# Entry of a hybrid mLSTM/attention kernel: latent norm factors first, dummy products moved, modulation columns amid a tile's products

## The chip, the cores and the metric

One NeuronCore of one Trainium2 chip runs the program. The metric is device time in microseconds of one execution; the median of three executions of the kernel before is 1206.87 us (1203.84 to 1209.22).

## What is computed

Two layers over 512 latent tokens and 256 context tokens with 1024 features: layer 0 is a bidirectional chunkwise mLSTM, layer 1 a banded windowed attention with sinks. Each layer first normalises and modulates its input, then projects it. For the entry of layer 0, which is all that the change touches, the reference is:

```python
mod_lat = jax.nn.silu(c) @ ada_w[layer] + ada_b[layer]
mod_ctx = jax.nn.silu(c_ctx) @ ada_w[layer] + ada_b[layer]
sh_l, sc_l, g_l = jnp.split(mod_lat[:, None, :], 3, axis=-1)
sh_c, sc_c, g_c = jnp.split(mod_ctx[None, None, :], 3, axis=-1)
h_lat = modulate(x, norm_g[layer], sh_l, sc_l)
h_ctx = modulate(ctx, norm_g[layer], sh_c, sc_c)
...
def rms_norm(a, g):
    af = af * lax.rsqrt(jnp.mean(af * af, axis=-1, keepdims=True) + EPS)
def modulate(a, g, shift, scale):
    return rms_norm(a, g) * (1 + scale) + shift
...
q, k, v, o, z, g = jnp.split(h @ w_in, ML_SPLITS, axis=-1)
```

## The kernel before

Features lie on the partitions and tokens on the free dimension. The input stands in eight feature tiles `x[j]` of 128 features by 768 tokens (`T`), of which 512 are latent (`TL`) and 256 context. Products are made in three passes of two-part numbers (`mm3`, line 188): high weight by high input, high by low, low by high. `HL` holds the modulated latent input in both parts, `HC` that of the context.

A scheduler sets the order of instructions on each engine from the order in the source and its own costs; `after(...)` (line 181) holds an instruction back until a named one has been issued. Each engine then works through its own list in that order, and SP issues the transfers.

The entry goes in these steps.

- **Dummies and sums of squares** (lines 246 to 265). `warm` runs products of zeros on TensorE, 36 of them into `pstat`. ScalarE squares the tiles, VectorE adds the squares in three groups of tiles, (0 to 3), (4, 5), (6, 7), and a product with `ones` sums each group over the partitions into `pstat`.
- **Norm factors** (`rs`, line 271, and `rsqrt`, line 194): one scale-and-add on VectorE, `Ln` and `Exp` on ScalarE, then three VectorE operations that refine the root. It is done for the 512 latent tokens (`rs(0, TL)`) and the 256 context tokens (`rs(TL, T)`), and gives `rstd`.
- **Modulation of layer 0** (`mod_quarter`, line 216). The vectors of two feature tiles (a quarter) come at once. Eight products with `ccol` make *rows* (line 221) from four 512 KB pieces of `ada0`, ScalarE copies the rows to `rt` (line 223), four products with `sel2` turn them into *columns* (line 225), and three small VectorE operations (lines 228 to 231) write shift and scale to `modc`. Quarter 0 is made before the first tile; quarter `c` is made ahead of tile `j = 1, 3, 5`, for the tiles after it.
- **Tiles** (line 307). For each `j`, VectorE multiplies `x[j]` by `rstd` (`xr`, line 314), ScalarE applies scale and shift (line 284) and casts to the high part (line 100), VectorE subtracts for the low part (line 106), and TensorE makes 12 latent products of 512 columns and 12 context products of 256 columns for the q and k weights of head 0 (lines 192 and 331), in three PSUM tiles `pqk`.
- **Gates** (lines 333 to 335): 48 products into `pgate`. VectorE's long gate chain (from line 362) starts with the last of them.

The weights come as `wraw` (SP), are cast to `whi` by ScalarE (line 100), and `wlo` is subtracted by VectorE (line 106), so ScalarE and VectorE do the weights' work in the same lists as the entry's own. `wraw` has two buffers: SP's third load of it waits until VectorE has made the first `wlo`.

A second lot of `warm`, 8 dummies into the first `pqk` (line 292), stands in TensorE's list between the sums of the first group and those of the second.

Of the kernel before, what the change touches and what calls it, by code (L numbers as in the profile page):

```python
# [8 lines left out]
F32 = mybir.dt.float32  # L9
# [7 lines left out]
P = 128  # L17
D = 1024
KT = D // P
TL = 512  # L20
TC = 256
T = TL + TC
# [4 lines left out]
NEG = -30000.0  # L27
BIG = -(2.0**100)

WARM, WARM2 = 36, 8  # L30


HEAD0 = "ooodommommommommodd"
# [31 lines left out]
def hybrid_kernel(ctx: ExitStack, tc: tile.TileContext, a: dict, out: bass.AP, dbg=None):  # L65
    nc = tc.nc
    ve, se, ge, te, sy = nc.vector, nc.scalar, nc.gpsimd, nc.tensor, nc.sync
# [8 lines left out]
    def mk(pool, shape, dt, tag, bufs=1, name=None):  # L76
        cnt[0] += 1
        return pool.tile(shape, dt, tag=tag, bufs=bufs, name=f"{name or tag}{cnt[0]}")
# [4 lines left out]
    def t0(shape, dt, tag, bufs=1):  # L83
        return mk(sb0, shape, dt, tag, bufs)

    def big(name):
        return mk(ps0, [P, 1024], F32, "big", 3, name)

    def ch(name):
        return mk(ps0, [P, 1024], F32, "ch", 1, name)  # L90

    def tmp(n=T, dt=F32):
        return t0([P, n], dt, "tmp", 5)

# [32 lines left out]
    def load_x(small=()):  # L127
        xs = [t_([P, 4, T], F32, n) for n in ("xa", "xb")]
        for j in range(KT):
            sy.dma_start(xs[j // 4][:, j % 4], a["xin"][:, j])  # L130
            for dst, src in small[j : j + 1]:
                sy.dma_start(dst, src)
        return xs, [xs[j // 4][:, j % 4] for j in range(KT)]

    _, x = load_x(small)
# [12 lines left out]
    st0 = [ada0(0)]  # L148
# [12 lines left out]
    sel2 = t0([P, 2], F32, "sel2")  # L161
# [19 lines left out]
    def after(*insts):  # L181

        st = ExitStack()
        for i in insts:
            st.enter_context(tc.issue_after(getattr(i, "ins", i)))
        return st

    def mm3(outs, w, ms, first, last):

        for i, (s, m) in enumerate(PASSES):  # L190
            for o, mv in zip(outs, ms):
                te.matmul(o, w[s], mv[m], start=first and i == 0, stop=last and i == 2)  # L192

    def rsqrt(dst, v, y, w, prev=None, tiny=0.0):

# [17 lines left out]
                out=junk, in0=src, in1=c2[:, v], scale=1.0, scalar=0.0,  # L213
                op0=ALU.mult, op1=ALU.add, accum_out=modc[:, layer, part, j, v : v + 1])

    def mod_quarter(R, srcs, c):


        for kk in range(2):
            for g in range(4):  # L220
                te.matmul(R[32 * g : 32 * g + 32], ccol[:, 4 * kk + g], srcs[4 * kk + g], start=kk == 0, stop=kk == 1)
        rt = tmp()[:, 0:TL]
        se.copy(rt, R)
        for q in range(4):
            te.matmul(R[:, 2 * q : 2 * q + 2], rt[:, q * P : (q + 1) * P], sel2, start=True, stop=True)
        js = slice(2 * c, 2 * c + 2)
        p4 = R[:, 0:8].rearrange("p (r j v) -> p r j v", r=2, v=2)
        ve.tensor_add(modc[:, 0, 0, js], p4[:, 0], adab[:, 0, 0, js, None].to_broadcast([P, 2, 2]))
        m = modc[:, 0, 1, js]
        ve.tensor_add(m, p4[:, 1], bp1[:, 0, js, None].to_broadcast([P, 2, 2]))  # L230
        ve.tensor_mul(m, m, ng[:, 0, js, None].to_broadcast([P, 2, 2]))

    HL = HC = None

# [11 lines left out]
    def warm(dst, n):  # L246
        for _ in range(n):
            te.matmul(dst[:, 0:TL], zeror, zeror[:, None, :].to_broadcast([P, 4, P]), start=True, stop=True)

    warm(pst, WARM)  # L250
    lastadd = []
    for js in ((0, 1, 2, 3), (4, 5), (6, 7)):
        for j in js:
            q = tmp()
            lastsq = se.activation(q, x[j], AF.Square)
            if j == 1:
                se.activation(csil, csil, AF.Silu)
                ve.tensor_copy(ccol[:, :, 0:2], csil.rearrange("p v k -> p k v"))
            if j == js[0]:
                ss = q  # L260
            else:
                with after(*lastadd):
                    lastadd = [ve.tensor_add(ss, ss, q)]
        for l, r in ((0, TL), (TL, T)):
            laststat = te.matmul(pst[:, l:r], ones, ss[:, l:r], start=(j == 3), stop=(j == 7))
    with after(*lastadd):
        ve.tensor_scalar(bp1, adab[:, :, 1], 1.0, None, op0=ALU.add)
    rstd = t0([P, T], F32, "bc0")
    v_, y_, w_ = tmp(), tmp(), tmp()

    def rs(l, r, prev=None):
        ve.tensor_scalar(v_[:, l:r], pst[:, l:r], 1.0 / D, EPS, op0=ALU.mult, op1=ALU.add)
        return rsqrt(rstd[:, l:r], v_[:, l:r], y_[:, l:r], w_[:, l:r], prev)

    rstd_exp, _ = rs(0, TL, lastsq)
    rs(TL, T)
    R = ch("R")
    mod_quarter(R[:, 0:TL], st0[0], 0)
    HL = t_([P, 2, KT, TL], F32R, "HL")
    HC = t_([P, 2, KT, TC], F32R, "HC")  # L280

    def enter(j, v, xr, hf):
        l, r = ((0, TL), (TL, T))[v]
        se.activation(hf[:, l:r], xr[:, l:r], AF.Identity,
                      scale=modc[:, 0, 1, j, v : v + 1], bias=modc[:, 0, 0, j, v : v + 1])
        dst = (HL, HC)[v]
        split(hf[:, l:r], dst[:, 0, j], dst[:, 1, j])

    wgt = t0([P, 3072], F32R, "s")
    acc = [big("pqk") for _ in range(3)]  # L290
    pbw = t0([P, 1024], F32R, "pb")
    warm(acc[0], WARM2)
    wq = [[load_w(a["w0"][0, u, 0]), None] for u in range(2)]
    st0.append(ada0(1))
    wq[0][1] = load_w(a["w0"][0, 0, 1])
# [10 lines left out]
    lastmm = None  # L306
    for j in range(KT):
        if j % 2 and j < KT - 1:

            c = j // 2 + 1  # L310
            with after(lastmm):
                mod_quarter(R[:, c % 2 * TL : c % 2 * TL + TL], st0[c], c)
        xr, hf = tmp(), tmp()
        ve.tensor_mul(xr, x[j], rstd)
        enter(j, 0, xr, hf)
        enter(j, 1, xr, hf)
        st, sp = j == 0, j == KT - 1
        hl, hc = hparts(j)
        wj = [[[wq[u][j // 4][m][:, j % 4, f * P : (f + 1) * P] for m in range(2)] for f in range(2)] for u in range(2)]
        for u in range(2):  # L320
            for f in range(2):
                mm3((acc[u][:, f * TL : (f + 1) * TL],), wj[u][f], [hl], st, sp)
        if j == 0:

            for u in range(2):
                te.matmul(acc[2][:, u * TL : (u + 1) * TL], zeror, zeror[:, None, :].to_broadcast([P, 4, P]),
                          start=True, stop=False)
        for u in (1, 0):
            for f in range(2):
                for i, (wi, m) in enumerate(PASSES):  # L330
                    lastmm = te.matmul(acc[2][:, u * TL + f * TC : u * TL + (f + 1) * TC], wj[u][f][wi], hc[m],
                                       start=False, stop=sp and f == 1 and i == 2)
# [361 lines left out]
    s = scores(qk)  # L694
# [39 lines left out]
    first = [gates.last, scores.last]  # L734
    for what in HEAD0:
# [25 lines left out]
    for h in range(1, NH0):  # L761
# [3 lines left out]
        s = scores(qk)  # L765
# [62 lines left out]
    for u in range(4):  # L828
        hi, lo = (w3a[:, 2 * u], w3a[:, 2 * u + 1]) if u < 3 else (w3b[:, 0], w3b[:, 1])
# [450 lines left out]
```

## Time and profile before

| what | value |
|---|---|
| median of 3 executions | 1206.87 us (1203.84 to 1209.22) |
| the profiled execution's own time | 1208.84 us |
| its span in the trace | 1207.0 us |
| mean granted TensorE clock | 0.983 |
| TensorE products, busy | 1151.3 us (95%) |
| VectorE, ScalarE, GpSimd, busy | 766.9, 541.1, 230.1 us |

The profiled execution lies 1.97 us above the median. The first 88 us, up to the last gate product, hold the steps above. Busy time of an engine is the time in which at least one of its instructions ran; the granted clock is 1.00 at 2.4 GHz and 0.50 at 1.2 GHz. In lists by time, a row gives the start, the duration, the engine and line, and in brackets the idle time of the engine before it with what ended that idle time; the durations of instructions that follow each other overlap a little.

### The profile page before, as it was taken

What the parts mean: (1) busy time and instruction counts of PE and PEld (TensorE: products, weight loads), DVE (VectorE), ACT (ScalarE), POOL (GpSimd) and SP (SyncE); (2) the same over time, 40 slices, a digit from 0 to 9 for tenths busy, and PEclk for the clock granted to TensorE, in tenths of its full rate; (3) what the DMA queues carried; (4) which work ended last, traced back from release to release, by engine and by line L of the source; (5) the groups of instructions that cost most, each with busy time, mean ns of one, the idle gap of its engine ahead of it and who ended that gap; (6) DMA issues with size and microseconds to landing.
All of it is one profiled execution on the core that took longest, in us unless ns stands there. A gap on an engine that the chain in (4) does not pass through costs nothing. (4 is left out here: it accounts for less than half of the span.)

```text
span 1207.0 us, 15997 instructions
## 1 busy us (share of the span) xinstructions
PE 1151.3 (95%) x6289; PEld 972.6 (81%) x6289; DVE 766.9 (64%) x1184; ACT 541.1 (45%) x901; POOL 230.1 (19%) x203
## 2 busy tenths in 40 slices
PE   7898899999999999999999999999999799998997
PEld 5677788888878888887888887888998587776776
DVE  4438878174845941582863367274777287979886
ACT  5443523343444232433423333443675277765663
POOL 0010520143201102211200330110233214123220
PEclk9998899999999999999999999999999899999999
DMA  8522522232215322221532112324108722225002
GB/s 311 196 70 70 199 77 74 79 102 81 81 53 182 111 70 71 71 66 47 201 122 70 60 55 70 122 70 123 53 21 170 189 84 65 70 71 140 18 18 70
DMA packets 38459, 116.90 MB, mean 97 GB/s; under 512 B 5088, under 2 KB 9328, under 8 KB 37360
## 3 DMA queue, kind: packets, MB, share of 16 engines
q1 hardware_dynamic: 35568, 108.55, 27.4%
q0 software_dynamic: 2816, 7.34, 3.4%
q8 instruction: 49, 0.80, 0.3%
q14 instruction: 26, 0.21, 0.1%
HBM read 107.60 MB, written 8.27 MB: 96 GB/s over the span
## 5 line engine op out<-in xcount | busy, mean ns | idle before, releaser
L100 ACT CAST whi<-wraw 128x1024 fp32r<-128x1024 f32 x102 | 107.0, 1052 | 202.6 <-PE pwo L192 51.4
L106 POOL TENSOR_TENSOR wlo<-wraw,whi 128x1024 fp32r<-128x1024 f32 x31 | 75.3, 2436 | 278.5 <-ACT whi L100 269.6
L106 DVE TENSOR_TENSOR wlo<-wraw,whi 128x1024 fp32r<-128x1024 f32 x71 | 87.5, 1234 | 54.0 <-ACT whi L100 54.0
L192 PE MATMUL po<-HL,whi 128*128 128x512 f32 x256 | 96.9, 402 | 0.0
L192 PE MATMUL pz<-HL,whi 128*128 128x512 f32 x256 | 96.3, 400 | 0.0
L192 PE MATMUL pqk<-HL,whi 128*128 128x512 f32 x240 | 90.3, 410 | 5.6 <-ACT HL L100 5.2
L192 PE MATMUL pv<-whi,HL 128*128 128x512 f32 x256 | 83.1, 391 | 0.0
L192 PE MATMUL po<-HC,whi 128*128 128x256 f32 x256 | 72.3, 282 | 0.0
L192 PE MATMUL pz<-HC,whi 128*128 128x256 f32 x256 | 71.9, 281 | 0.0
L192 PE MATMUL Lq<-HL,whi 128*128 128x512 f32 (+1 forms) x192 | 55.8, 370 | 6.2 <-DVE szt L1047 6.2
L1115 PE MATMUL Lpv<-PT,V 128*128 128x512 f32 x144 | 54.4, 430 | 7.2 <-DVE PT L106 6.0
L192 PEld LDWEIGHTS pqk<-HL,whi 128*128 128x128 f32 x240 | 46.1, 195 | 18.0 <-ACT HL L100 5.5
L192 PEld LDWEIGHTS po<-HL,whi 128*128 128x128 f32 x256 | 48.8, 190 | 12.6
L192 PEld LDWEIGHTS pz<-HL,whi 128*128 128x128 f32 x256 | 48.5, 190 | 12.4
L192 PEld LDWEIGHTS pv<-whi,HL 128*128 128x128 f32 x256 | 48.1, 188 | 11.3 <-DVE vgb L106 1.2
L614 POOL TENSOR_TENSOR tmp<-tmp,tmp 128x768 f32<-128x768 f32 x8 | 14.7, 1838 | 212.4 <-ACT tmp L613 212.4
L192 PE MATMUL pqk<-HC,whi 128*128 128x256 f32 x192 | 53.6, 279 | 0.0
L1080 DVE TENSOR_REDUCE negm<-Lsc 128x2 f32<-128x1024 f32 (+1 forms) x32 | 43.4, 1355 | 14.5 <-PE Lsc L1078 13.7
L212 DVE CUSTOM_DVE_ANT_0 junk<-qkp 128x1024 bf16<-128x1024 f32 x40 | 48.7, 1218 | 5.1 <-DMA qkp<-ada 4.6
L192 PE MATMUL po<-HL,wlo 128*128 128x512 f32 x128 | 51.8, 405 | 0.0
L192 PE MATMUL pz<-HL,wlo 128*128 128x512 f32 x128 | 51.6, 403 | 0.0
L106 DVE TENSOR_TENSOR PT<-LT,PT 128x512 fp32r<-128x512 f32 x72 | 48.9, 684 | 4.2 <-ACT PT L100 3.9
(388 smaller groups left out, 3247.3 us busy)
## 6 DMA issues: line engine op xcount, KB each, us to landing
wraw<-w SPq DMA_DIRECT2D x85, 512.0 KB, 3.6
qkp<-ada SPq DMA_DIRECT2D x30, 512.0 KB, 5.5
wraw<-wo SPq DMA_DIRECT2D x24, 512.0 KB, 3.5
vgb<-ada SPq DMA_DIRECT2D x9, 512.0 KB, 7.3
vga<-ada SPq DMA_DIRECT2D x8, 512.0 KB, 8.5
Q<-hl POOLq DMA_DIRECT2D x8, 512.0 KB, 5.5
xa<-xin SPq DMA_DIRECT2D x8, 384.0 KB, 4.2
xb<-xin SPq DMA_DIRECT2D x8, 384.0 KB, 6.3
```

Of the source, the lines that this page charges most:

```text
L100: se.copy(dst, src)
L106: return (le or ve).tensor_sub(lo, src, f32(hi))
L192: te.matmul(o, w[s], mv[m], start=first and i == 0, stop=last and i == 2)
L212: ve.tensor_tensor_reduce(out=junk, in0=src, in1=c2[:, v], scale=1.0, scalar=0.0, op0=ALU.mult, op1=ALU.add, accum_out=modc[:, layer, part ...
L614: (ge if e < 3 else ve).tensor_add(ss, ss, sq)
L1080: ve.tensor_reduce(nmx[:, 0, 2 * p2 : 2 * p2 + 2], both, axis=AX.X, op=ALU.max, negate=True)
L1115: te.matmul(po, V[:, kb, g], hl[:, m], start=(bi == 0 and m == 0), stop=(bi == len(blocks) - 1 and m == 1))
```

## The change

It does five things.

- `rs(0, TL)` stays where it is in the source, `rs(TL, T)` goes behind the first tile's latent input: the factors of the context are held back by `after(xr0, hi_0)`. The latent part of `xr` for tile 0 is a multiplication of its own (512 columns).
- The sums of squares go in two groups of four tiles, in place of three.
- `mod_quarter` is cut into `mod_rows` (rows and the copy) and `mod_cols` (columns and `modc`). Quarter 0 has a PSUM tile of its own, `R0`, of the kind that `pqk` uses.
- For `j = 1, 3, 5`, `mod_cols` is issued behind the first unit's (q) six latent products of that tile, in place of ahead of the tile.
- The second dummies are 16 in place of 8, and stand behind the columns of quarter 0.

```diff
-WARM, WARM2 = 36, 8
+WARM, WARM2 = 36, 16
...
-    def mod_quarter(R, srcs, c):
+    def mod_rows(R, srcs):
...
         rt = tmp()[:, 0:TL]
         se.copy(rt, R)
+        return rt
+
+    def mod_cols(R, rt, c):
+
         for q in range(4):
-            te.matmul(R[:, 2 * q : 2 * q + 2], rt[:, q * P : (q + 1) * P], sel2, start=True, stop=True)
+            mm = te.matmul(R[:, 2 * q : 2 * q + 2], rt[:, q * P : (q + 1) * P], sel2, start=True, stop=True)
...
+        return mm
...
-    for js in ((0, 1, 2, 3), (4, 5), (6, 7)):
+    for js in ((0, 1, 2, 3), (4, 5, 6, 7)):
...
+    R0 = big("R0")[:, 0:TL]
+    rt = mod_rows(R0, st0[0])
     rstd_exp, _ = rs(0, TL, lastsq)
-    rs(TL, T)
-    R = ch("R")
-    mod_quarter(R[:, 0:TL], st0[0], 0)
+    xr_0, hf_0 = tmp(), t0([P, T], F32, "rowt")
+    xr0 = ve.tensor_mul(xr_0[:, 0:TL], x[0][:, 0:TL], rstd[:, 0:TL])
+    cols0 = mod_cols(R0, rt, 0)
...
-        split(hf[:, l:r], dst[:, 0, j], dst[:, 1, j])
+        hi = se.copy(dst[:, 0, j], hf[:, l:r])
+        ve.tensor_sub(dst[:, 1, j], hf[:, l:r], f32(dst[:, 0, j]))
+        return hi
+
+    hi_0 = enter(0, 0, xr_0, hf_0)
+    with after(xr0, hi_0):
+        rs(TL, T)
+        ve.tensor_mul(xr_0[:, TL:T], x[0][:, TL:T], rstd[:, TL:T])
+        enter(0, 1, xr_0, hf_0)
...
-    warm(acc[0], WARM2)
+    with after(cols0):
+        warm(acc[0], WARM2)
+    R = ch("R")
+    R = [R[:, 0:TL], R[:, TL : 2 * TL]]
...
             with after(lastmm):
-                mod_quarter(R[:, c % 2 * TL : c % 2 * TL + TL], st0[c], c)
-        xr, hf = tmp(), tmp()
-        ve.tensor_mul(xr, x[j], rstd)
-        enter(j, 0, xr, hf)
-        enter(j, 1, xr, hf)
+                rt = mod_rows(R[c % 2], st0[c])
+        if j:
+            xr, hf = tmp(), tmp()
+            ve.tensor_mul(xr, x[j], rstd)
+            enter(j, 0, xr, hf)
+            enter(j, 1, xr, hf)
...
-                mm3((acc[u][:, f * TL : (f + 1) * TL],), wj[u][f], [hl], st, sp)
+                lastmm = mm3((acc[u][:, f * TL : (f + 1) * TL],), wj[u][f], [hl], st, sp)
+            if not u and j % 2 and j < KT - 1:
+                with after(lastmm):
+                    mod_cols(R[c % 2], rt, c)
```

From the last gate product on, the lists of all engines hold the same instructions in the same order as before, and SP's and GpSimd's lists are the same throughout. What moves stands at three places.

**Place 1, ScalarE's list from the load of its table to the first tile's latent input.** The table is that of `Ln` and `Exp`; `R_199` and `R_185` are the rows of quarter 0, `tmp_184` and `tmp_183` the root, `tmp_271` and `rowt_204` the modulated tile 0. Before:

```order
L199 ACT_TABLE_LOAD
L201 ACTIVATE tmp_184<-tmp_183 128x512
L203 ACTIVATE tmp_184<-tmp_183 128x256
L204 ACTIVATE tmp_184<-tmp_184 128x512
L204 ACTIVATE tmp_184<-tmp_184 128x256
L223 COPY tmp_208<-R_199 128x512
L100 CAST whi_234<-wraw_232 128x1024
L284 ACTIVATE tmp_271<-tmp_270,modc_113 128x512
L100 CAST whi_240<-wraw_238 128x1024
L100 CAST HL_217<-tmp_271 128x512
```

And now:

```order
L200 ACT_TABLE_LOAD
L224 COPY tmp_194<-R_185 128x512
L100 CAST whi_252<-wraw_250 128x1024
L202 ACTIVATE tmp_183<-tmp_182 128x512
L205 ACTIVATE tmp_183<-tmp_183 128x512
L100 CAST whi_258<-wraw_256 128x1024
L292 ACTIVATE rowt_204<-tmp_203,modc_113 128x512
L295 CAST HL_213<-rowt_204 128x512
L204 ACTIVATE tmp_183<-tmp_182 128x256
L205 ACTIVATE tmp_183<-tmp_183 128x256
```

`Ln` and `Exp` of the latent tokens (lines 202 and 205) now stand behind the copy of the rows and behind the first weight's cast; those of the context come behind the latent input.

VectorE's list at the same place, from the first scale-and-add of the factors. Before:

```order
L272 TENSOR_SCALAR tmp_183<-pstat_115 128x512
L272 TENSOR_SCALAR tmp_183<-pstat_115 128x256
L205 TENSOR_TENSOR tmp_185<-tmp_184 128x512
L205 TENSOR_TENSOR tmp_185<-tmp_184 128x256
L206 SCALAR_TENSOR_TENSOR tmp_185<-tmp_185,tmp_183 128x512
L206 SCALAR_TENSOR_TENSOR tmp_185<-tmp_185,tmp_183 128x256
L207 SCALAR_TENSOR_TENSOR bc_182<-tmp_185,tmp_184 128x512
L207 SCALAR_TENSOR_TENSOR bc_182<-tmp_185,tmp_184 128x256
L228 TENSOR_TENSOR modc_113<-R_199,adab_72 128x4
L230 TENSOR_TENSOR modc_113<-R_199,bp_114 128x4
L314 TENSOR_TENSOR tmp_270<-xa_76,bc_182 128x768
L231 TENSOR_TENSOR modc_113<-modc_113,ng_73 128x4
```

And now:

```order
L278 TENSOR_SCALAR tmp_182<-pstat_115 128x512
L233 TENSOR_TENSOR modc_113<-R_185,adab_72 128x4
L235 TENSOR_TENSOR modc_113<-R_185,bp_114 128x4
L236 TENSOR_TENSOR modc_113<-modc_113,ng_73 128x4
L106 TENSOR_TENSOR wlo_253<-wraw_250,whi_252 128x1024
L206 TENSOR_TENSOR tmp_184<-tmp_183 128x512
L207 SCALAR_TENSOR_TENSOR tmp_184<-tmp_184,tmp_182 128x512
L106 TENSOR_TENSOR wlo_259<-wraw_256,whi_258 128x1024
L208 SCALAR_TENSOR_TENSOR bc_181<-tmp_184,tmp_183 128x512
L285 TENSOR_TENSOR tmp_203<-xa_76,bc_181 128x512
L278 TENSOR_SCALAR tmp_182<-pstat_115 128x256
L296 TENSOR_TENSOR HL_213<-rowt_204,HL_213 128x512
```

`modc` and two low weight parts (`wlo`) now stand ahead of the end of the root (line 208) and of `xr` (line 285); before, both `wlo` came behind them.

**Place 2, TensorE's list between tile 0 and tile 1, and ScalarE's beside it.** `R_199` and `R_249` are the rows of quarter 1. TensorE before:

```order
L221 MATMUL R_199<-vgb_67,ccol_71 32x512 x4
L221 MATMUL R_199<-qkp_68,ccol_71 32x512 x4
L225 MATMUL R_199<-sel_109,tmp_313 128x2 x4
L192 MATMUL pqk_220<-HL_217,whi_234 128x512
L192 MATMUL pqk_221<-HL_217,whi_240 128x512
L331 MATMUL pqk_222<-HC_218,whi_240 128x256
L192 MATMUL pqk_220<-HL_217,whi_234 128x512
```

And now:

```order
L222 MATMUL R_249<-vgb_67,ccol_71 32x512 x4
L222 MATMUL R_249<-qkp_68,ccol_71 32x512 x4
L192 MATMUL pqk_229<-HL_213,whi_252 128x512
L192 MATMUL pqk_230<-HL_213,whi_258 128x512
L354 MATMUL pqk_231<-HC_214,whi_258 128x256
L192 MATMUL pqk_229<-HL_213,whi_252 128x512
L192 MATMUL pqk_229<-HL_213,wlo_253 128x512
L192 MATMUL pqk_229<-HL_213,whi_252 128x512 x2
L192 MATMUL pqk_229<-HL_213,wlo_253 128x512
L230 MATMUL R_249<-sel_109,tmp_322 128x2 x4
L192 MATMUL pqk_230<-HL_213,whi_258 128x512
```

ScalarE before:

```order
L223 COPY tmp_313<-R_199 128x512
L284 ACTIVATE tmp_323<-tmp_322,modc_113 128x512
L284 ACTIVATE tmp_323<-tmp_322,modc_113 128x256
L100 CAST HL_217<-tmp_323 128x512
L100 CAST HC_218<-tmp_323 128x256
```

And now:

```order
L224 COPY tmp_322<-R_249 128x512
L292 ACTIVATE tmp_325<-tmp_324,modc_113 128x512
L100 CAST s_228<-wraw_276 128x1024
L295 CAST HL_213<-tmp_325 128x512
L292 ACTIVATE tmp_325<-tmp_324,modc_113 128x256
L295 CAST HC_214<-tmp_325 128x256
```

The four column products moved from ahead of tile 1's products to among them. On ScalarE the copy of the rows still stands ahead of tile 1's input, and a weight's cast now stands inside it.

**Place 3, TensorE's list between tile 4 and tile 5.** `R_199` and `R_249` are now the rows of quarter 3. Before:

```order
L221 MATMUL R_199<-vga_66,ccol_71 32x512 x6
L225 MATMUL R_199<-sel_109,tmp_479 128x2 x4
L192 MATMUL pgate_587<-HL_217,s_219 128x512
L192 MATMUL pgate_587<-HC_218,s_219 128x256
L192 MATMUL pgate_587<-HL_217,s_219 128x512
L192 MATMUL pgate_587<-HC_218,s_219 128x256
L192 MATMUL pgate_587<-HL_217,s_219 128x512
L192 MATMUL pgate_587<-HC_218,s_219 128x256
L192 MATMUL pgate_587<-HL_217,s_219 128x512
L192 MATMUL pgate_587<-HC_218,s_219 128x256
L192 MATMUL pgate_587<-HL_217,s_219 128x512
L192 MATMUL pqk_220<-HL_217,whi_250 128x512
```

And now:

```order
L222 MATMUL R_249<-vga_66,ccol_71 32x512 x6
L192 MATMUL pqk_229<-HL_213,whi_268 128x512
L192 MATMUL pqk_230<-HL_213,s_228 128x512
L354 MATMUL pqk_231<-HC_214,s_228 128x256
L192 MATMUL pqk_229<-HL_213,whi_268 128x512
```

Nine of the gate products that stood in this place now stand behind tile 5 or tile 7.

## Rows read from the trace of the kernel before

**Rows 1.** Page, part 1: busy time of TensorE's products over the span.

```profile
PE 1151.3 (95%) x6289; PEld 972.6 (81%) x6289; DVE 766.9 (64%) x1184; ACT 541.1 (45%) x901; POOL 230.1 (19%) x203
```

**Rows 2.** Windows by stretch: start:end, length, busy of each engine, clock, DMA share, GB/s.

```profile
27.48:34.36 6.88, 6.88 (x26) 5.45 (x26) 3.72 (x5) 1.90 (x3) 0.00 (x0) 0.69 0.98 385
34.36:38.70 4.34, 2.98 (x25) 1.39 (x25) 0.55 (x3) 2.35 (x5) 0.00 (x0) 0.99 1.02 412
38.70:48.90 10.20, 10.20 (x48) 8.48 (x48) 5.91 (x9) 4.37 (x7) 0.00 (x0) 0.84 0.62 227
48.90:53.24 4.34, 2.98 (x25) 1.39 (x25) 0.55 (x3) 2.35 (x5) 0.00 (x0) 1.00 0.02 9
53.24:62.54 9.30, 8.88 (x48) 7.42 (x48) 3.46 (x7) 4.38 (x7) 3.80 (x2) 1.00 0.05 8
```

**Rows 3.** Timeline of TensorE's products, first 70 us.

```profile
13.97 2.20 PE L248 MATMUL pqk<-zeror 128*128 128x512 f32 x8
...
21.19 0.60 PE L221 MATMUL R<-vgb,ccol 128*32 128x512 f32 x2
22.52 1.05 PE L225 MATMUL R<-sel,tmp 128*128 128x2 f32 x8 [0.73 <-ACT tmp L223]
27.48 1.22 PE L192 MATMUL pqk<-HL,whi 128*128 128x512 f32 x2 [3.91 <-ACT HL L100]
...
36.99 1.05 PE L225 MATMUL R<-sel,tmp 128*128 128x2 f32 x8 [0.70 <-ACT tmp L223]
38.70 1.22 PE L192 MATMUL pqk<-HL,whi 128*128 128x512 f32 x2 [0.66 <-ACT HL L100]
...
53.24 0.74 PE L192 MATMUL pqk<-HL,whi 128*128 128x512 f32 x2 [0.66 <-ACT HL L100]
...
54.52 0.49 PE L192 MATMUL pqk<-HL,whi 128*128 128x512 f32 x1 [0.42 <-DVE HL L106]
...
65.17 1.05 PE L225 MATMUL R<-sel,tmp 128*128 128x2 f32 x8 [0.70 <-ACT tmp L223]
66.71 0.47 PE L192 MATMUL pgate<-HL,s 128*128 128x512 f32 x1 [0.49 <-DVE modc L230]
...
68.42 0.40 PE L192 MATMUL pqk<-HL,whi 128*128 128x512 f32 x1
```

**Rows 4.** Timeline of ScalarE, same stretch.

```profile
19.58 0.63 ACT L201 ACTIVATE tmp<-tmp 128x512 f32<-128x512 f32 x1 [2.68 <-DVE tmp L272]
...
21.88 0.58 ACT L223 COPY tmp<-R 128x512 f32<-128x512 f32 x1 [0.55 <-PE R L221]
22.36 1.05 ACT L100 CAST whi<-wraw 128x1024 fp32r<-128x1024 f32 x1
25.16 0.81 ACT L284 ACTIVATE tmp<-tmp,modc 128x512 f32<-128x512 f32 x1 [1.75 <-DVE modc L231]
...
26.82 0.61 ACT L100 CAST HL<-tmp 128x512 fp32r<-128x512 f32 x1
...
36.35 0.58 ACT L223 COPY tmp<-R 128x512 f32<-128x512 f32 x1 [5.41 <-PE R L221]
36.84 1.30 ACT L284 ACTIVATE tmp<-tmp,modc 128x512 f32<-128x512 f32 x2
```

**Rows 5.** Timeline of VectorE, same stretch.

```profile
24.96 1.22 DVE L106 TENSOR_TENSOR wlo<-wraw,whi 128x1024 fp32r<-128x1024 f32 x1
...
28.09 0.68 DVE L106 TENSOR_TENSOR HL<-tmp,HL 128x512 fp32r<-128x512 f32 x1
```

**Rows 6.** Transfers issued at 10.66 us: count, KB each, us from issue to landing.

```profile
vgb<-ada SPq DMA_DIRECT2D x1, 512.0 KB, 9.1
```

**Rows 7.** Timeline of TensorE behind the gates.

```profile
105.09 0.90 PE L406 MATMUL pgt<-ident,vgb 64*128 64x64 f32 x6 [4.02 <-DVE vgb L390]
```

**Rows 8.** Timeline of TensorE's weight loads at the columns of quarter 1.

```profile
36.99 0.97 PEld L225 LDWEIGHTS R<-sel,tmp 128*128 128x128 f32 x8 [1.61 <-ACT tmp L223]
```

More of the change, by code (lines that the diff above doesn't have):

```diff
@@ L191, in mm3 @@
             for o, mv in zip(outs, ms):
-                te.matmul(o, w[s], mv[m], start=first and i == 0, stop=last and i == 2)
+                mm = te.matmul(o, w[s], mv[m], start=first and i == 0, stop=last and i == 2)
+        return mm
     def rsqrt(dst, v, y, w, prev=None, tiny=0.0):
@@ L231, in mod_quarter @@
         ve.tensor_mul(m, m, ng[:, 0, js, None].to_broadcast([P, 2, 2]))
+        return mm
     HL = HC = None
```

## Prediction

> **What bounds the kernel now.** I read the page's busy times first: TensorE's products fill 95% of the span [rows 1], so what shortens or lengthens TensorE's stay in the entry should reach the end. The change touches nothing behind the last gate product, so I then cut the entry into stretches by the windows view [rows 2], and looked in the timelines of TensorE, ScalarE and VectorE at what ended each pause [rows 3 to 5].
>
> Three things are to be seen. First, before tile 0 TensorE stands 3.91 us and waits for ScalarE's cast of `HL` [rows 3]. Second, the tiles do not run at one speed: the granted clock is 0.69 over tile 0, 0.84 over tiles 1 and 2, 1.00 over tiles 3 and 4 [rows 2]. Taken off at full clock, that is 6.88 x 0.31 = 2.1 us in tile 0 and 10.20 x 0.16 = 1.6 us in tiles 1 and 2. Both times it fell to 1.2 GHz towards the end of the pause ahead (0.99 over the stretch ahead of tile 1), and rose again within the tiles. Third, each later quarter costs one stretch of 4.34 us from its first row product to the tile's first product [rows 2]: rows 1.92, a pause of 0.70, columns 1.05, a pause of 0.66 [rows 3]. In that stretch ScalarE is never free: its copy starts as the rows end, then come the two modulations of the tile (1.30) [rows 4] and the cast, and tile products wait for that cast. So the columns lie in a time in which TensorE would wait anyway.
>
> **The way to tile 0.** The new order puts the factors ahead in the source, but ScalarE's list has the copy of the rows and a weight's cast ahead of `Ln`. Before, `Ln` ran at 19.58, ahead of the copy at 21.88 [rows 4]. The copy needs the rows, and these need the fourth piece of `ada0`, issued at 10.66 and landed 9.1 later, at 19.8 [rows 6]. Its two products (0.60 each [rows 3]) end at 20.9. Then follow copy 0.58 to 21.6 and cast 1.05 to 22.6; this cast had no wait before at 22.36 [rows 4], so its data come by then, which allows up to 0.8 more. `Ln` 0.63 and an `Exp` taken as long end at 23.8. On VectorE the columns (1.05 from 21.6) and `modc` are done at 23.0, then the first `wlo` takes 1.22 to 24.2 [rows 5], two root operations of 512 columns (0.68 each, as the subtraction of that size [rows 5]) run to 25.6, the second `wlo` to 26.8, the last root operation and `xr` to 28.1. Consecutive rows overlap by some 0.1, so 27.7. ScalarE's 0.81 and 0.61 [rows 4] give the first product at **29.2 in place of 27.48: +1.7**. It could be +0.4, if one `wlo` falls into a wait, or +2.5 with the late cast. I take +1.7, since all its terms are rows.
>
> Two more terms belong to tile 0. The second product now needs the low part of `HL`, 0.68 behind the high one [rows 5]; before, two other products stood between. That is 0.45 of waiting. And the dummies: 8 took 2.04 to the next product, 0.25 each [rows 3], so 16 run from 22.7 to 26.7, and the idle pause ahead of tile 0 shrinks from 3.91 to 2.5. They cost nothing, as TensorE waits behind them anyway. If the clock holds through this pause, tile 0 gets 2.1 back: 1.7 + 0.45 - 2.1 = **0.0**.
>
> The shorter sums (two groups in place of three) and the context's factors cost nothing: the rows wait for the piece at 19.8, and the context's input has tile 0's latent products as cover. At full clock a tile takes (9.30 - 0.42) / 2 = 4.4 [rows 2, 3], and two thirds of its columns are latent, so the cover is 0.45 + 3.0. The context's own chain, with the same operations at half the width (0.4 each) and one weight's cast, is some 4 from the end of the latent cast, by my estimate: if the cover is short, up to 0.5 shows. SP's third weight load, which waits for the first `wlo` (done at 26.2 before [rows 5], at 24.2 now), goes 2 us earlier. Nothing on TensorE waited for it, so I cost it at nothing.
>
> **Tile 1.** ScalarE keeps the copy ahead of the modulation and now has a weight's cast of 1.05 in the place of one context modulation (0.5): **+0.5**. The low part comes behind that cast's own subtraction on VectorE, as `pb` stands ahead of it: another 0.45 of waiting. The columns, now among the products, add 1.05. At full clock the stretch of tiles 1 and 2 loses its 1.6: 0.45 + 1.05 - 1.6 = **-0.1**.
>
> **Tile 3.** The pause stays, 0.70 + 1.05 + 0.66 = 2.4, only empty; the columns come on top, +1.05. VectorE has no `modc` ahead of the low part any more, so most of the 0.42 wait at 54.52 goes [rows 3]: **+0.7**.
>
> **Tile 5.** Before, 3.95 lay between the rows and the first product at 68.42, of which nine gate products from 66.71 made 1.71 useful [rows 3]: 2.24 lost. Now 2.4 empty, 1.05 of columns and 0.1 of waiting, 3.55: **+1.3**.
>
> Sum with a full clock throughout: 0.0 + 0.5 - 0.1 + 0.7 + 1.3 = **+2.4 us**.
>
> The price of the columns is bounded by one row: eight records took 1.05 with nothing beside them, and their loads 0.97 of it [rows 8]. The Trainium skill (TensorE: Matmul & The Clock Gate, Step-by-step: what each phase is for) says that weight loads are pulled ahead of running products. By it the columns would cost 0.08 in place of 1.05 per quarter. I keep 1.05: only the first load has a long product to hide under.
>
> **The clock** decides the rest. Four pauses of 2.4 to 2.9 us are now wholly empty of products, where three of them held 1.05 of columns. Before, a stretch with 1.36 of empty time and these columns lost the clock once (ahead of tile 1) and kept it once (ahead of tile 3) [rows 2]. An empty pause can hardly do better, so each of the four loses it with about even chance, at 1.6 us a fall, the row of tiles 1 and 2. The waits for low parts are partly hidden in a slow stretch, about 0.2 a fall. Two falls: +2.4 + 3.2 - 0.4 = **+5.2**. The Trainium skill (same page, What's actually happening) says that the gate's timer does not restart with a kernel; by it one program keeps its clock in some executions and loses it in others.
>
> The profiled execution took 1208.84 us, 1.97 above the median; I add the sum to the median: **1212.1 us**, 0.43% slower. What this kernel's measurement can tell from no change is about 0.5%, or 6 us.
>
> **Rivals.**
> - *The clock falls in three or all four pauses*: +2.4 + 4 x 1.6 - 0.8 = +8, 1215 us (three: 1213.5). For it: the pauses are empty. Against: the same length kept its clock ahead of tile 3. Slower by over 0.5%.
> - *It falls at most once*: +2.4 to +3.8, 1209.3 to 1210.7. For it: 16 dummies, and 2.5 is less than 3.91.
> - *The other side: the factors really come early.* If VectorE's two `wlo` and ScalarE's casts fall into waits, the chain ends with the copy at 21.6 and the columns, and only `xr` (0.68), 0.81 and 0.61 follow `modc` at 23.0: first product at 25.1, -2.4 in place of +1.7. With a full clock that is +2.4 - 4.1 = -1.7, **1205.2 us**, faster than before. It decides at one point: whether `Ln` of the latent tokens runs ahead of the copy of the rows. The list of ScalarE speaks against it.
> - *The columns are hidden amid the products*: 3 x 0.97 less, +5.2 - 2.9 = +2.3, 1209.2 us. Against: each of the eight loads has only a product of two columns ahead of it, and [rows 8] shows them one behind the other. This is the case of the page named above under the columns.
> - *The shift does not reach the end.* 4.02 us of TensorE's time ahead of 105.09 wait for VectorE's gate chain [rows 7]. Were that chain fixed in time, a later entry would be absorbed and the time be 1207. But the chain starts with the last gate product, so it moves along.
>
> **How the numbers follow.** Two falls 0.38; three or four 0.28; at most one 0.16; factors early 0.08; columns hidden 0.07; not reaching the end 0.03. The three executions shown lie up to 3 us from their median, and I add that to the ends: from 1209.3 - 3 to 1215 + 3, so 1206 to 1218. Slower by over 0.5% (above 1212.9) hold the second case and a fifth of the first: 0.36. Faster by over 0.5% (below 1200.8) none of them gives; 0.03 is left for what I did not see. The rest, 0.61, is within 0.5%.
>
> **What would show it.** Right: `Ln` at about 22.6 behind a weight's cast; the first tile product at 29 (28 to 30); three empty pauses of 2.4 to 2.9 between rows and tile products; columns of about 1 us among the products; the last gate product 2 to 8 us later than before. Wrong: `Ln` ahead of the copy; a first product before 27; pauses shorter than 2; or a granted clock of 1.00 through all four pauses, and a time at or below 1207.

## The result, and the profile after

The changed kernel takes 1219.5 us (median of 6, 1216.49 to 1222.22), the kernel before 1206.58 us (median of 6, 1203.84 to 1209.22): ratio 1.0108, 95% interval 1.0095 to 1.0122. That is 12.9 us slower. Its profiled execution took 1217.48 us over a span of 1215.7; the pair of profiled executions differs by 8.6 us.

The windows of the kernel after, cut at the same events as [rows 2], with one more behind them: from the rows of quarter 3 to the last gate product. Columns as there: the ratio behind the five engines is the granted clock.

```profile
28.19:35.13 6.94, 6.71 (x27) 5.25 (x27) 5.64 (x9) 2.62 (x5) 0.00 (x0) 0.75 1.03 412
35.13:39.92 4.79, 1.92 (x17) 0.41 (x16) 0.54 (x1) 2.80 (x5) 0.00 (x0) 1.00 0.76 303
39.92:51.50 11.58, 11.51 (x57) 9.34 (x57) 6.01 (x11) 3.93 (x7) 0.00 (x0) 0.85 0.25 63
51.50:55.83 4.33, 1.92 (x17) 0.41 (x16) 0.02 (x1) 2.34 (x5) 0.00 (x0) 1.00 0.19 76
55.83:68.62 12.79, 12.79 (x57) 11.09 (x57) 4.17 (x9) 4.48 (x7) 4.41 (x2) 0.73 0.05 6
68.62:98.44 29.82, 27.41 (x146) 22.74 (x146) 9.66 (x19) 11.33 (x22) 0.94 (x1) 0.89 0.21 69
```

The kernel before has this last stretch too:

```profile
62.54:87.99 25.45, 24.26 (x146) 20.08 (x146) 10.35 (x20) 11.34 (x22) 0.95 (x1) 1.00 0.25 81
```

Against [rows 2], stretch by stretch, the last gate product ends 10.45 us later:

| stretch | before | after | difference | clock before, after |
|---|---|---|---|---|
| start to tile 0's first product | 27.48 | 28.19 | +0.71 | |
| tile 0 | 6.88 | 6.94 | +0.06 | 0.69, 0.75 |
| rows of quarter 1 to tile 1 | 4.34 | 4.79 | +0.45 | 0.99, 1.00 |
| tiles 1 and 2 | 10.20 | 11.58 | +1.38 | 0.84, 0.85 |
| rows of quarter 2 to tile 3 | 4.34 | 4.33 | 0 | 1.00, 1.00 |
| tiles 3 and 4 | 9.30 | 12.79 | +3.49 | 1.00, 0.73 |
| rows of quarter 3 to the last gate product | 25.45 | 29.82 | +4.37 | 1.00, 0.89 |

Three quarters of it lie where the clock was 1.00 before and is not now. Length times the missing clock gives what it took: before 2.1 and 1.6 us (tile 0, tile 1); after 1.7, 1.7, 3.5 (12.79 x 0.27) and 3.3 (29.82 x 0.11). So 10.2 in place of 3.8, 6.4 of the 10.45 us.

The falls of the clock are not of one size. Two stretches at 0.50 after the change, at tiles 1 and 3:

```profile
40.36:43.77 3.41, 3.34 (x10) 2.31 (x8) 1.19 (x3) 0.42 (x2) 0.00 (x0) 0.50 0.57 154
57.42:64.25 6.83, 6.83 (x27) 6.16 (x26) 2.45 (x7) 3.16 (x5) 0.04 (x1) 0.50 0.01 2
```

And the one at tile 0 before it:

```profile
24.96:31.79 6.83, 4.31 (x10) 3.24 (x11) 4.20 (x7) 4.22 (x6) 0.00 (x0) 0.50 0.71 257
```

After the change the clock stood at 0.50 for 3.4 us at tile 0 (30.12 to 33.53) and at tile 1, and for 6.8 us at tile 3 and at tile 5 (74.49 to 81.32), although TensorE was busy. Half of each is lost, 1.7 or 3.4 us. The kernel before has a fall of the long kind too. It began 1.4 us into the pause ahead of tile 0, and 2.5 of its 6.8 us lay in that pause, so only 2.1 show in tile 0.

TensorE's products after, by time; the lines answer to [rows 3] and [rows 7].

```profile
18.38 1.05 PE L222 MATMUL R<-vgb,ccol 128*32 128x512 f32 x4
20.11 1.05 PE L230 MATMUL R<-sel,tmp 128*128 128x2 f32 x8 [0.69 <-ACT tmp L224]
21.03 3.90 PE L254 MATMUL pqk<-zeror 128*128 128x512 f32 x16
28.19 0.50 PE L192 MATMUL pqk<-HL,whi 128*128 128x512 f32 x1 [3.26 <-ACT HL L295]
28.91 0.50 PE L192 MATMUL pqk<-HL,whi 128*128 128x512 f32 x1 [0.23 <-DVE HL L296]
...
39.92 0.88 PE L192 MATMUL pqk<-HL,whi 128*128 128x512 f32 x2 [2.87 <-ACT HL L295]
...
43.56 1.05 PE L230 MATMUL R<-sel,tmp 128*128 128x2 f32 x8
...
55.83 0.74 PE L192 MATMUL pqk<-HL,whi 128*128 128x512 f32 x2 [2.41 <-ACT HL L295]
...
58.15 1.71 PE L230 MATMUL R<-sel,tmp 128*128 128x2 f32 x8
...
72.95 0.50 PE L192 MATMUL pqk<-HL,whi 128*128 128x512 f32 x1 [2.41 <-ACT HL L295]
...
115.55 0.90 PE L429 MATMUL pgt<-ident,vgb 64*128 64x64 f32 x6 [4.01 <-DVE vgb L413]
```

The pauses ahead of tiles 1, 3 and 5 are there whole, 2.87, 2.41 and 2.41 us, and the columns now lie amid the products; in tiles 3 and 5 they run at the low clock (1.71 and 1.70 in place of 1.05). The gate chain moves along: its wait is 4.01 as it was 4.02 [rows 7].

ScalarE after, the way to tile 0 and tile 1's input [rows 4].

```profile
19.48 0.59 ACT L224 COPY tmp<-R 128x512 f32<-128x512 f32 x1 [4.04 <-PE R L222]
19.96 1.05 ACT L100 CAST whi<-wraw 128x1024 fp32r<-128x1024 f32 x1
20.91 0.63 ACT L202 ACTIVATE tmp<-tmp 128x512 f32<-128x512 f32 x1
...
26.67 0.81 ACT L292 ACTIVATE rowt<-tmp,modc 128x512 f32<-128x512 f32 x1 [3.53 <-DVE tmp L285]
...
37.60 0.81 ACT L292 ACTIVATE tmp<-tmp,modc 128x512 f32<-128x512 f32 x1
38.32 1.03 ACT L100 CAST s<-wraw 128x1024 fp32r<-128x1024 f32 x1
39.25 0.62 ACT L295 CAST HL<-tmp 128x512 fp32r<-128x512 f32 x1
```

VectorE after, the same stretch [rows 5].

```profile
21.62 1.23 DVE L106 TENSOR_TENSOR wlo<-wraw,whi 128x1024 fp32r<-128x1024 f32 x1
...
24.09 1.22 DVE L106 TENSOR_TENSOR wlo<-wraw,whi 128x1024 fp32r<-128x1024 f32 x1
25.23 0.68 DVE L208 SCALAR_TENSOR_TENSOR bc<-tmp,tmp 128x512 f32<-128x512 f32 x1
```

`Ln` ran only behind the copy and a cast, though the engine had stood idle for 4.04 us ahead of that copy; both `wlo` ran inside the root.

From the gates on, both kernels do the same. Of the 10.45 us the profiled pair still has 9.9 near the end: one subtraction of VectorE starts at 1189.99 before and at 1199.93 after. Another 1.3 go in the last stretch, where the kernel before alone lost the clock in the middle (0.72 from 1195 to 1201). The windows of this same work, first before, then after:

```profile
1190.00:1207.00 17.00, 10.86 (x71) 10.30 (x71) 8.22 (x18) 1.60 (x4) 0.66 (x1) 0.87 0.32 106
```

```profile
1200.00:1215.70 15.70, 9.55 (x71) 8.83 (x71) 8.18 (x18) 1.55 (x4) 0.60 (x1) 0.96 0.34 113
```

That is most of why the pair differs by 8.6 at the end and by 10.45 at the gates. Below, an effect inside the entry is read from the end of the last gate product (**gate end**: 87.99 before, 98.44 after), the whole from the medians of several executions.

### The profile page after: what moved, and what is told of

Its sections match the earlier page's. It is cut to its first block, busy times and chain, and to the rows that moved or that the text cites. A ratio compares the mean times of both kernels' runs of the same rounds, so it can differ in the third digit from the quotient of the medians.

```text
span 1215.7 us, 16000 instructions
## 1 busy us (share of the span) xinstructions
PE 1157.3 (95%) x6293; PEld 976.3 (80%) x6293; DVE 767.0 (63%) x1186; ACT 541.6 (45%) x901; POOL 231.8 (19%) x203
```

## The experiments

The theory that they test: the emptied pauses lose TensorE's clock, and that is most of the loss. The rivals: the new way to tile 0; the columns' own time and the lost gate products. Each ratio and difference is taken against the kernel before as measured again beside the run (medians of 1204.85 to 1206.78 us); clocks, waits and gate ends are those of one profiled execution each.

**e1 and e2: each half of the change alone.** e1 is the kernel before with only this:

```diff
             with after(lastmm):
-                mod_quarter(R[:, c % 2 * TL : c % 2 * TL + TL], st0[c], c)
+                rt = mod_rows(R[:, c % 2 * TL : c % 2 * TL + TL], st0[c])
...
+            if not u and j % 2 and j < KT - 1:
+                with after(lastmm):
+                    mod_cols(R[:, c % 2 * TL : c % 2 * TL + TL], rt, c)
```

> The kernel before with one part of the change: the columns of quarters 1 to 3 go amid the products of tiles 1, 3 and 5; the way to tile 0 (factors, dummies, sums) is the old one. Theory (emptied pauses lose the clock): first tile product at 27.5 as before; the three pauses ahead of tiles 1, 3 and 5 are 2.4 to 2.9 us and empty; at least two stretches behind them show a granted clock below 0.90; last gate product 96 to 99 us (before 88.0); time 1214 to 1219 us. Rival 1 (the new way to tile 0 is the cause): last gate product within 2 us of before, time at most 1209. Rival 2 (only the columns' 1.05 us each and the lost gate products cost): +2.5 to +4 us and a clock as before, 1209 to 1211.

Measured: 1213.61 us, ratio 1.0062 (1.0044 to 1.0081), +7.7; gate end 91.09. The windows of e1's tiles: 0; 1 and 2; 3 and 4; 5 to the gates.

```profile
26.41:32.71 6.30, 6.29 (x26) 5.02 (x26) 4.59 (x6) 1.91 (x3) 0.00 (x0) 0.75 0.96 382
...
37.05:48.80 11.75, 11.75 (x72) 8.77 (x72) 6.54 (x11) 4.34 (x7) 0.00 (x0) 1.00 0.62 217
51.23:63.20 11.97, 11.72 (x72) 8.71 (x72) 6.37 (x9) 4.28 (x7) 5.37 (x2) 1.00 0.11 32
65.59:88.00 22.41, 22.41 (x112) 19.57 (x113) 9.53 (x19) 8.99 (x18) 0.00 (x0) 0.85 0.15 57
```

All three pauses were 2.41 us, and here only the one ahead of tile 5 lost the clock (22.41 x 0.15 = 3.4 us). The theory asked for at least two slow stretches and a gate end of 96 to 99: both missed in this execution, and its time is just out of range. Both rivals' times (1209, 1211) are below the interval, 1211.2 to 1215.7.

e2 is the changed kernel with the columns back:

```diff
                 rt = mod_rows(R[c % 2], st0[c])
+                mod_cols(R[c % 2], rt, c)
...
-            if not u and j % 2 and j < KT - 1:
-                with after(lastmm):
-                    mod_cols(R[c % 2], rt, c)
```

> The changed kernel with the columns of quarters 1 to 3 put back behind their rows, ahead of tiles 1, 3 and 5; the new way to tile 0 stays. Theory (emptied pauses lose the clock): the columns cut each pause in two again and the gate products fill the one of tile 5; clock 1.00 over tiles 3 and 5; first product at 28.2, last gate product 87 to 90 us; time 1206 to 1210 us. Rival 1 (the way to tile 0 is the cause): the 10 us stay, 1215 to 1220.

Measured: 1211.98 us, ratio 1.0050 (1.0032 to 1.0069), +6.1; gate end 93.36. A miss on both sides: the way to tile 0 costs far more than the 0.8 us by which the first product is late, and less than all. The theory's clock of 1.00 missed at tile 3. The windows of e2's tile 0, tiles 1 and 2, tiles 3 and 4, and TensorE's waits at tile 1:

```profile
28.27:35.92 7.65, 7.65 (x27) 5.92 (x27) 4.78 (x8) 2.62 (x5) 0.00 (x0) 0.63 1.02 410
40.71:53.00 12.29, 11.47 (x48) 9.21 (x48) 5.36 (x9) 3.82 (x7) 0.00 (x0) 0.72 0.30 85
57.40:68.00 10.60, 10.36 (x52) 8.42 (x56) 3.45 (x7) 4.37 (x7) 3.90 (x2) 0.84 0.04 13
```

```profile
40.71 1.13 PE L192 MATMUL pqk<-HL,whi 128*128 128x512 f32 x2 [1.11 <-ACT HL L295]
42.67 0.80 PE L192 MATMUL pqk<-HL,whi 128*128 128x512 f32 x1 [0.82 <-DVE HL L296]
```

The missing clock took 2.8, 3.4 and 1.7 us, 8.0 in place of 3.8 before: so most of this half's loss (5.4 us at the gates) is the clock as well. Tile 1 waits 1.11 and 0.82 where it waited 0.66 and none, for ScalarE's cast of a weight into `s` stands inside its entry. The two halves come to 7.7 + 6.1 = 13.8, against 12.9; as the falls differ from kernel to kernel, that they add up is in part chance.

**e3: the pauses filled with dummies.** The changed kernel, and:

```diff
-                rt = mod_rows(R[c % 2], st0[c])
+                rt, lastrow = mod_rows(R[c % 2], st0[c])
+            with after(lastrow):
+                warm(R[(c + 1) % 2], 8)
```

> The changed kernel with 8 more products of zeros (512 columns each, into the free half of R) behind the rows of each of quarters 1 to 3, so 24 products are added whose results nobody reads. They take about 2 us of each pause of 2.4 to 2.9. Theory (clock): the granted clock stays at 1.00 over tiles 3 and 5, the stretches fall by some 3.4 us each, last gate product at 89 to 93 us, time 1208 to 1213 us. Rival 2 (columns amid products and the lost filler cost, not the clock): last gate product stays at 97 to 99, time 1217 to 1222.

Measured: 1210.83 us, ratio 1.0037 (1.0025 to 1.0050); gate end 91.11, 7.33 earlier than after the change. Windows of e3 (tile 0; then from each lot of dummies on), and TensorE around the second lot:

```profile
27.99:34.91 6.92, 6.70 (x26) 5.25 (x27) 5.64 (x9) 2.63 (x5) 0.00 (x0) 0.75 1.03 409
37.54:52.00 14.46, 14.17 (x80) 10.20 (x80) 6.55 (x11) 6.09 (x10) 0.00 (x0) 1.00 0.34 109
52.79:66.20 13.41, 13.41 (x80) 10.28 (x80) 6.39 (x9) 6.00 (x10) 5.09 (x2) 1.00 0.08 23
67.01:88.00 20.99, 20.99 (x119) 18.35 (x120) 9.54 (x19) 10.71 (x21) 0.00 (x0) 1.00 0.23 73
```

```profile
52.79 2.11 PE L254 MATMUL R<-zeror 128*128 128x512 f32 x8 [0.70 <-ACT tmp L224]
54.74 0.62 PE L192 MATMUL pqk<-HL,whi 128*128 128x512 f32 x2
```

Nothing but useless products was added, and the time fell from +12.9 to +4.9 over the kernel before. With 24 dummies the clock is 1.00 from tile 1 to the gates. So some 8 of the 12.9 us are the clock in these pauses: shown.

**e4: no pauses.** The changed kernel with a tile's input issued ahead of the rows:

```diff
     for j in range(KT):
+        if j:
+            xr, hf = tmp(), tmp()
+            ve.tensor_mul(xr, x[j], rstd)
+            enter(j, 0, xr, hf)
+            enter(j, 1, xr, hf)
         if j % 2 and j < KT - 1:
...
                 rt = mod_rows(R[c % 2], st0[c])
-        if j:
...
```

> The changed kernel with the input of tiles 1, 3 and 5 issued ahead of their quarter's rows, so that ScalarE makes it during the tile before and its copy of the rows comes behind; nothing is added or left out. Theory (the pauses, and the clock lost in them, are the cost): no pause over 0.5 us ahead of tiles 1, 3 and 5, clock 1.00 from tile 1 to the gates, last gate product at 82 to 87 us; time 1200 to 1206 us, faster than both. Rival 2 (columns amid products are what costs): they now wait for the copy, 1 us or more each, time 1212 or more. Rival 3 (the shift at the gates is taken up later): gate end earlier, time within 2 us of before.

Measured: 1201.69 us, ratio 0.9963 (0.9949 to 0.9978); gate end 82.00. From the rows of quarter 1 to the last gate product TensorE is busy throughout and the clock is 1.00:

```profile
34.97:82.00 47.03, 47.03 (x290) 37.44 (x290) 19.72 (x38) 22.61 (x40) 5.17 (x2) 1.00 0.29 100
```

The pauses came from ScalarE's copy of the rows ahead of the tile's input, which needs none of these rows: quarter `c` serves the tiles behind.

**e5: the columns' price.** e4 with each column product of quarters 1 to 3 made twice:

```diff
-        for q in range(4):
+        for q in range(4 if c == 0 else 8):
+            q %= 4
```

> The kernel of e4 (input of tiles 1, 3 and 5 ahead of the rows) with the four column products of quarters 1 to 3 made twice, 12 products of two columns more, same result. It prices the columns amid products where no clock is lost. My prediction's price (1.05 us for four, on the path): last gate product 82.0 + 3 x 0.95 = 84.9 us, time +2.9 us over e4, 1204.5. Rival (weight loads are pulled ahead under the tile's products, 0.08 each): last gate product 82.0 to 82.4, time as e4, 1201.7.

Measured: 1205.38 us, ratio 0.9986 (0.9968 to 1.0003); gate end 84.19, first product 27.85 (e4: 28.05). One quarter's columns in e4, then in e5:

```profile
38.34 0.95 PE L230 MATMUL R<-sel,tmp 128*128 128x2 f32 x8
39.15 0.72 PE L192 MATMUL pqk<-HL,whi 128*128 128x512 f32 x2
```

```profile
37.91 1.84 PE L231 MATMUL R<-sel,tmp 128*128 128x2 f32 x16
```

(84.19 - 27.85) - (82.00 - 28.05) = 2.39 us for 12 products more: 0.80 us per quarter. The added columns stand behind other columns; but the four of e4 take as much between long products, 0.81 from their start to the next product's. The time is 2.8 us above e4's, each against its kernel before. The rival of hidden columns falls.

**e6: e4 with the old way to tile 0** (e1, with the same move of the tile's input as in e4).

> The kernel of e1 (the kernel before with only the columns amid the products) and the input of tiles 1, 3 and 5 issued ahead of their rows, so as e4 but with the old way to tile 0: factors of latent and context tokens together, 8 dummies ahead of the second sums. Theory (the pauses cost; the new way to tile 0 buys nothing): no pause ahead of tiles 1, 3 and 5, last gate product 81 to 83 us, time 1200 to 1203 us, as e4. Rival (the new way to tile 0 gains behind its own cost): 1205 or more. If the new way to tile 0 costs by itself what e2 showed (+6 us): 1196 to 1198.

Measured: 1201.51 us, ratio 0.9947 (0.9933 to 0.9960); gate end 82.37, first product 26.20. The two ways to tile 0 can't be told apart here. The new one starts 1.85 us later (28.05 in e4) and has it back by the gates: tile 4 waits 0.48 and 0.50 us in e6 (the expectation of e10 calls it tile 3), and the clock over tile 0 is 0.54 (26.20 to 33.09) against e4's 0.75 (28.05 to 34.97), some 1.4 us. So e2's 6.1 us are not a fixed price of the new way: without the pauses it costs nothing that shows.

**e7: e2 without the cast inside tile 1's entry.** The two lots of weights into `s` are split behind `hi` of tile 1:

```diff
-    split(raw, wgt[:, 2048:3072], pbw)
+    raw1 = raw
...
-    split(raw, wgt[:, 0:1024], wgt[:, 1024:2048])
+    raw2 = raw
...
+            if j == 1:
+                with after(hi):
+                    split(raw1, wgt[:, 2048:3072], pbw)
+                    split(raw2, wgt[:, 0:1024], wgt[:, 1024:2048])
```

> The kernel of e2 (columns back ahead of the tiles, new way to tile 0) with the two casts of weights into the tile s held until tile 1's latent input is cast; nothing is added or left out. In e2 tile 1 waited 1.11 us for the cast of HL and 0.82 for its low part, where the kernel before had 0.66 and none, and the clock fell over it. Theory (ScalarE's cast of 1.05 inside tile 1's entry makes e2's loss): the pauses of tile 1 are 0.66 and at most 0.2 again, last gate product 88 to 91 us, time 1206 to 1209. Rival (the later first product and the dummies make it): time stays at 1211 to 1213.

Measured: 1209.64 us, ratio 1.0022 (1.0010 to 1.0033); gate end 89.95, against 93.36 in e2. The waits of tile 1:

```profile
40.28 0.73 PE L192 MATMUL pqk<-HL,whi 128*128 128x512 f32 x2 [0.66 <-ACT HL L295]
...
41.56 0.79 PE L192 MATMUL pqk<-HL,whi 128*128 128x512 f32 x1 [0.43 <-DVE HL L296]
```

The gate end is the theory's, the time just above its range, and the second wait is longer than the 0.2 that it allowed. Without the cast inside the entry some 3 us of e2's loss are gone (6.1 - 2.9; 3.4 at the gates). The two waits shrank by 0.84 together; the larger part is the clock, which in e7 is 0.84 over tiles 1 and 2 and 1.00 over tiles 3 and 4, in place of 0.72 and 0.84. Some 3 us stay with the rest of the way to tile 0.

**e8: dummies up to tile 0.** e4 with `WARM2` at 28.

> The kernel of e4 with 28 dummies behind the columns of quarter 0 in place of 16, so that they reach to the first tile product (16 take 3.9 us, and 3.2 us of pause were left). Theory (the pause ahead of tile 0 costs the clock in tile 0, some 1.7 us): granted clock 1.00 over tile 0, first product at 28.0 to 28.3, last gate product 80.0 to 80.6 us, time 1199 to 1201 us. Rival (the clock falls for another reason, or the dummies push the first product): first product later than 28.5 or clock 0.75 over tile 0, time 1202 or more.

Measured: 1201.33 us, ratio 0.9952 (0.9939 to 0.9965); gate end 81.62. The clock over tile 0 is 1.00 now, as the theory had it, yet only 0.4 us of the 1.7 come back at the gates, so gate end and time miss its ranges. TensorE in e8's tile 0:

```profile
32.71 0.84 PE L354 MATMUL pqk<-HC,whi 128*128 128x256 f32 x2 [1.14 <-ACT HC L295]
```

The faster tile runs into the context's input, whose factors the change put behind the latent ones: 1.14 us of waiting that the slow clock had covered.

**e9: `Ln` where the source has it.** e4, with ScalarE's copy of quarter 0's rows and the first two weights held back:

```diff
-    rt = mod_rows(R0, st0[0])
     rstd_exp, _ = rs(0, TL, lastsq)
+    rt = mod_rows(R0, st0[0], rstd_exp)
...
-    wq = [[load_w(a["w0"][0, u, 0]), None] for u in range(2)]
+    with after(rstd_exp):
+        wq = [[load_w(a["w0"][0, u, 0]), None] for u in range(2)]
```

> The kernel of e4 with ScalarE's Ln and Exp of the latent tokens put ahead of the copy of quarter 0's rows and of the first weight's cast, which both wait for them in the list; the order that the change's source has. It tests the step of the prediction that put the first tile product at 29.2 and the rival 'factors really early' (25.1). Theory (the place of Ln in ScalarE's list sets the first product): Ln at 17.5 to 18.5, first tile product at 24.5 to 25.5 in place of 28.05, last gate product 78.5 to 80 (82.0), time 1198 to 1200 us. Rival (another chain, by the weights' casts or modc, ends as late): first product 27 or later, last gate product over 81, time 1201 to 1203.

Measured: 1197.78 us, ratio 0.9934 (0.9918 to 0.9950), the lowest median; gate end 78.70, first product 26.77. ScalarE in e9, and tile 0's window:

```profile
18.73 0.63 ACT L202 ACTIVATE tmp<-tmp 128x512 f32<-128x512 f32 x1 [2.52 <-DVE tmp L279]
...
21.47 0.58 ACT L225 COPY tmp<-R 128x512 f32<-128x512 f32 x1
...
25.51 0.62 ACT L296 CAST HL<-rowt 128x512 fp32r<-128x512 f32 x1
```

```profile
26.80:31.83 5.03, 5.00 (x28) 3.97 (x26) 4.09 (x8) 3.13 (x6) 0.00 (x0) 1.00 1.03 410
```

The first product comes 1.3 us earlier than in e4 (between the two theories: `HL` is ready at 26.1, and the dummies run to 26.9), and the 16 dummies now fill the pause: clock 1.00 over tile 0.

**e10 and e11: two tries at more.** e10 is e6 with 15 dummies behind quarter 0's columns (`with after(cols0)`) and the last split into `s` held behind tile 4's `hi`. e11 is e9 with the weights held behind the copy (`with after(cp0)`, `cp0` being that copy) and 12 dummies.

> The kernel of e6 (old way to tile 0, columns amid the products, inputs of tiles 1, 3 and 5 ahead of the rows) with 15 dummies behind the columns of quarter 0 in place of 8 ahead of the second sums, and the last of the weights' casts into the tile s held until tile 4's latent input is cast. Theory (the clock lost in tile 0 and the waits of 0.48 and 0.50 in tile 3 are what is left): granted clock 1.00 over tile 0, no wait over 0.3 us from there to the gates, last gate product 79 to 80.5 us (82.4), time 1198 to 1200 us. Rival (the clock in tile 0 gives nothing, as the context's input then ends the wait, which took 1.14 us in e8): last gate product 81.5 to 82.5, time 1201 to 1202.

> The kernel of e9 with the two casts of weights held behind the copy of quarter 0's rows (in e9 the copy stood behind a cast that waited for its transfer until 20.5 us), and 12 dummies in place of 16, as those of e9 ran 0.8 us past the cast of HL that the first product needs. Theory (ScalarE's order sets the first product): copy at 20 to 20.4, first tile product at 24.3 to 25.5 in place of 26.8, last gate product 77 to 78.5 us (78.7), time 1196 to 1198 us, the best of all. Rival (the low parts of weights and input on VectorE, now later, end the wait in its place): first product earlier, but last gate product 78.5 or later and time 1198 to 1200.

Measured: e10 1199.65 us, ratio 0.9956 (0.9940 to 0.9971), gate end 79.15; clock as full as expected, though tile 6 now waits 0.68 us. e11 1199.19 us, ratio 0.9942 (0.9926 to 0.9959), gate end 78.71: first product at 24.25, 2.5 us ahead of e9, and nothing of it left at the gates, as its rival had it (tile 0 waits 0.50 and tile 4 0.61 us for low parts of `HL`). e9, e10 and e11 can't be told apart.

## Why the prediction was wrong

It said slower, but by 5.2 us in place of 12.9, and put 0.61 on "within 0.5%". Step by step:

- **The clock: the step that failed.** The step "each of the four loses it with about even chance, at 1.6 us a fall" gave two falls, +3.2 - 0.4. All four pauses lost it, and the price was wrong too: 1.7 us at tiles 0 and 1, but 3.5 and 3.3 at tiles 3 and 5. I took the price from the row of tiles 1 and 2, whose fall lasted 3.4 us (38.62 to 42.03); the fall at tile 0, in the same trace, lasted 6.8. I read that one as beginning "towards the end of the pause", but it began 1.4 us into 3.91 (24.96). Where I took back 3.7 us (2.1 of tile 0, 1.6 of tile 1) and paid 2.8, the trace has 10.2 against 3.8. That is 7.3 us (6.4 + 3.7 - 2.8), against a miss of 7.7 in the medians and of 5.2 (10.45 - 5.2) at the gates of the profiled pair. The rival of three or four falls had the right event at the wrong price: with these prices it gives 2.4 + 10.2 - 0.8 = 11.8, or 1218.7 us.
- **The rest of the sum came within 2.0.** My terms without the clock come to 2.4 + 3.7 = 6.1, the profiled pair shows 10.45 - 6.4 = 4.1; the first product explains half of the difference. In e3, where only tile 0 loses the clock, my terms give 2.4 + 1.7 = 4.1; it stands at +4.9.
- **First product, +1.7**: it was +0.71 in the profiled pair. The fourth piece was issued at 9.55 after the change (its products at 18.38 end at 19.4, not 20.9), against 10.66 before [rows 6]. The old way in e1 issues it at 9.55 too, so that 1.1 us is not the change. Between the experiments, old way 26.41 and 26.20 (e1, e6), new way 27.85 to 28.27 (e2 to e5, e7, e8), the term is right, and so is its cause (e9).
- **16 dummies**: they left 3.26 us of pause and did not keep the clock (0.75), so tile 0 got 0.4 back, not 2.1. The pause was longer than the 2.5 I had, as the columns came 1.5 us earlier and the first product only 1.0.
- **Low part of tile 0, 0.45**: the wait was 0.23. **The context's input**: there was no wait in the change, and 1.14 us in e8 at full clock, more than the 0.5 I allowed.
- **Tile 1, +0.5**: it was +0.45, by the cast of `s` as said. But I costed the cast at its own length, and in e2 it goes with some 3 us (e7): it lengthens two waits, and the clock falls behind them. The same mistake as the first.
- **Tiles 3 and 5, +0.7 and +1.3**: without the clock's share the stretches grew by nothing (3.49 - 3.5) and by 1.1 (4.37 - 3.3).
- **Columns, 1.05 a quarter**: 0.80 (e5). The Trainium skill (TensorE: Matmul & The Clock Gate, Step-by-step: what each phase is for) has weight loads pulled ahead of running products. By it 0.08 would be left of a quarter's columns; 0.81 in e4 does not show that for these loads, and the measurement decides.
- **Pauses of 2.4**: they were 2.41 twice, and 2.87 ahead of tile 1. **Gates**: they move along, as said.
- **The other side, factors early (1205.2)**: e9 does it, in e4's frame, and the first product came at 26.8, not 25.1.

What stays open: why the clock stayed low twice as long at tiles 3 and 5 as at tiles 0 and 1 (in e2 and e7, whose way to tile 0 is the change's, it was 6.8 us at tile 0 as well), and why e1 kept the clock over two of three equal pauses. With e1 in view, that all four pauses lost it is in part chance. The Trainium skill (the same page, What's actually happening) says that the gate's timer runs free of the kernel; that agrees with e1, but no run here shows the timer.

## What to carry to other kernels

Cost an emptied pause of TensorE not by its length but by the clock that it can lose behind it, with the dearest fall that the trace shows: here 3.4 us for a pause of 2.4, and the trace before the change already held a fall of that length. Measure a fall from where the clock drops to where it rises, not by the tile that it ends in. Work moved out of a pause in which TensorE waits anyway saves nothing and may cost the cover; first take the pause itself away, by looking at what the waiting engine's list holds ahead of the awaited instruction (e4: a copy that the tile did not need; e9: a copy and a cast ahead of `Ln`). Issue order in the source is not the order on the engine, and a hold on one instruction sets it.

## What the runs showed of the hardware

- After the change the clock fell 0.4 to 1.9 us after the products had begun again behind each pause, and stayed at 0.50 for 3.4 us twice and 6.8 us twice; TensorE was busy for all of 57.42 to 64.25.
- Three equal pauses of 2.41 us in one execution (e1): the clock fell behind one and stayed behind two. In the change three of 2.41 to 2.87 all lost it.
- Products of zeros can keep the clock: eight of them in each pause, with 0.70 us idle ahead of them, left it at 1.00 (e3).
- Four products of two columns cost 0.80 us (e5), and 0.81 between long products (e4).
- A slow tile hides waits: at full clock tile 0 met a wait of 1.14 us that the change itself did not show (e8).
